# A softmax whose reciprocal sums are multiplied in by the transposing products, and pools that wait by tile

## Chip, cores and metric

The kernel runs on one core of a Trainium2 chip. The metric is the device time of one execution in microseconds (us). The core has five engines that work side by side, each through its own queue in order: TensorE (PE, the matrix products; PEld is its weight load), VectorE (DVE), ScalarE (ACT), GpSimd (POOL) and SyncE (SP, which here issues most transfers). An instruction starts when it is at the head of its queue and the semaphores that it waits for have been raised. Products write to PSUM, eight banks of 128 partitions x 512 fp32 values; DVE and ACT read them from there.

## What is computed

Two small networks over 512 tokens of width 1024, one after the other, in fp32: first a layer of a linear recurrence beside a long convolution, a feed-forward layer, a gated embedding, a windowed attention (16 heads) and again feed-forward and gate; then twice a layer with 8 heads of dilated and 8 of latent attention, followed by a feed-forward layer. The change concerns the softmax of the three attentions:

```python
pr = jax.nn.softmax(s.reshape(B, H, GRID_W, kh * kw), axis=-1)   # windowed
...
p = jnp.exp(s - m)                                               # dilated
l = jnp.sum(p, axis=-1, keepdims=True)
o = jnp.einsum('brhnij,brhnjd->brhnid', p, vw.astype(jnp.float32)) / l
...
p = jax.nn.softmax(s, axis=-1)                                   # latent
return jnp.einsum('bhqk,bkhd->bqhd', p.astype(v.dtype), v)
```

In the kernel the three dilated configurations are one dense attention with a bias that carries the distances, the masks and the weights of the mixture.

## The kernel before

Activations stand transposed, features on partitions and the 512 tokens along a row, as eight tiles `x[k]`. A large product (`gemm`) goes by output tiles of 128 features. For each it loads a weight tile `raw` through SP's queue; ACT rounds it to `wh` (L281), POOL takes the remainder `wl` (L282), and PE adds up three products for each 128 of depth, `wh` by the upper part of x, `wh` by its lower part, `wl` by the upper part (L292 to L294, in fp32r, a form of fp32 that goes over the array once). The result stands in a bank `ps_g`, and an evacuating function on DVE or ACT takes it away.

The stages follow in the order mix, mod, ffn.0, ple.0, na, setup2, ffn.1, ple.1, attn.0, mlp.0, attn.1, mlp.1. `na` is the windowed attention, `attn.0` and `attn.1` the dense layers. Each stage opens a pool of PSUM banks (`banks`, with a number of buffers for each kind: `g` for the large products, `a` for small ones; in attention also `s` scores, `t` transposed tiles, `o` outputs) and a pool in SBUF. A scheduler in the library sets the order on each engine from the order of the code, priorities and its own model of durations; it also makes the semaphores. By default the first tile that lies where an earlier pool lay waits for all of that pool to be released.

One softmax tile has 128 queries on partitions and up to 512 keys along a row. In `head` (dense layers) PE computes the scores into `ps_s`; DVE takes the maximum of each row `mx` (L1684, with the bias, or L1765); `probabilities` follows: DVE negates and scales the maximum (L1416), ACT takes the exponential into `e` and adds up each row into `sm` (L1418), DVE inverts `sm` (L1419), and `e` is multiplied by it, on DVE (L1425) for even tiles and on ACT (L1421) for odd ones. PE then transposes the four 128x128 blocks of `e` with the identity `ident` into `ps_t` (L1583), ACT rounds them to `pth` (L1584), DVE takes the remainder `ptl` (L1585), and PE multiplies with the values into `ps_o`. A dense layer has 16 heads of four such tiles. `na_head` does the same with tiles of 192 or 256 keys and two or three blocks (transposition at L1382), ten blocks a head. Between these PE has fillers: the products that the next heads need, or the output products `out2`. `cast_rows` (L1538) spreads a row of norms over 128 partitions with one product. `rms_of` does the same for the norm of x with a column of reciprocals, the identity as the moving operand (L357).

Of the kernel before, what the change touches and what calls it, by code (L numbers as in the profile page):

```python
# [9 lines left out]
F32 = mybir.dt.float32  # L10
# [7 lines left out]
P = 128  # L18
# [196 lines left out]
class Net:  # L215
    def __init__(self, ctx, tc, ins, at, out):
        self.tc, self.nc, self.ins, self.at, self.out = tc, tc.nc, ins, at, out
        self.bg = []
        pool = lambda name, **k: ctx.enter_context(tc.tile_pool(name=name, bufs=1, **k))
        self.const = pool("const")  # L220
        self.wp = pool("wp")
        self.xp = pool("xp")
        self.dram = pool("dram", space=bass.MemoryType.DRAM)
        nc = self.nc
        self.vecs = self.const.tile([P, ins["vecs"].shape[1]], F32, name="vecs")
        nc.sync.dma_start(self.vecs, ins["vecs"])
        self.ones = self.const.tile([P, P], F32, name="ones")
        nc.vector.memset(self.ones, 1.0)
        self.ident = self.const.tile([P, P], F32, name="ident")
        nc.sync.dma_start(self.ident, ins["ident"])  # L230
        self.weng = nc.gpsimd
        self.nw = 3
        self.ctx = ctx
        self.setup1()

    def make_x(self):
# [19 lines left out]
    @contextmanager  # L256
    def banks(self, **n):

        with self.tc.tile_pool(name="ps", bufs=1, space=PSUM) as self.ps:
            self.nb = n  # L260
            yield

# [113 lines left out]
    def ffn(self, i):  # L376
        nc, tc = self.nc, self.tc
        up, down = self.ins[f"ffn_up{i}"], self.ins[f"ffn_down{i}"]
        NF = DFF // P
        xs = self.scaled_parts(f"ffn_norm{i}")  # L380
        R, _ = self.rms()
        with tc.tile_pool(name=f"ffn{i}", bufs=1) as pool:
            def conv(o, m):
                u = pool.tile([P, S], F32, name="u", bufs=3)
                nc.vector.tensor_mul(u, o, R)
                c = pool.tile([P, S], F32, name="c", bufs=4)
                self.conv3(c, u, f"ffn{i}_c", f"ffn{i}_cb", m)
                return c

            for f0 in range(0, NF, 8):  # L390
                f1 = min(f0 + 8, NF)
                gs, held = [], {}

                def evac(m, o):
                    c = conv(o, m)
                    if m < NF:
                        nc.scalar.activation(c, c, AF.Gelu_apprx_tanh)
                        held[m] = c
                        return
                    gate = held.pop(m - NF)  # L400
                    nc.vector.tensor_mul(c, c, gate)
                    h = pool.tile([P, S], F32R, name="gh", bufs=10)
                    l = pool.tile([P, S], F32R, name="gl", bufs=10)
                    self.split(h, l, c)
                    gs.append((h, l))

                self.gemm(up, [m for f in range(f0, f1) for m in (f, f + NF)], xs, evac, lead=0 if f0 else 4)

                def add(m, o):
                    nc.vector.tensor_add(self.x[m], self.x[m], o)  # L410

                self.gemm(down, range(NKD), gs, add, f0, f1, tick=2)

    def ple(self, i):
        nc, tc = self.nc, self.tc
        with tc.tile_pool(name=f"ple{i}", bufs=1) as pool:
            p = pool.tile([P, 2, S], F32, name="p")
            nc.scalar.dma_start(p, self.ins[f"pT{i}"])
            ph = pool.tile([P, 2, S], F32R, name="ph")
            pl = pool.tile([P, 2, S], F32R, name="pl")  # L420
            self.split(ph, pl, p)
            xs = self.scaled_parts(f"ple_norm{i}")
            R, _ = self.rms()
            prj = {}

            def evac_p(m, o):
                prj[m] = o

            def evac(m, o):
                t = pool.tile([P, S], F32, name="t", bufs=3)  # L430
                nc.vector.tensor_mul(t, o, R)
                nc.scalar.activation(t, t, AF.Sigmoid)
                nc.vector.tensor_mul(t, t, prj.pop(m))
                nc.vector.tensor_add(self.x[m], self.x[m], t)

            psp = [(ph[:, k], pl[:, k]) for k in range(2)]
            for g in (range(2), range(2, 4), range(4, 6), range(6, 8)):
                self.gemm(self.ins[f"ple_proj{i}"], g, psp, evac_p)
                self.gemm(self.ins[f"ple_gate{i}"], g, xs, evac, lead=2)


    def mod(self):
        nc = self.nc
        const = self.ctx.enter_context(self.tc.tile_pool(name="mods", bufs=1))
        act = const.tile([P, NKD], F32, name="c_act")
        nc.scalar.activation(act, self.vecs[:, self.at["c"] : self.at["c"] + NKD], AF.Silu)
        self.mods = [const.tile([P, 6, NKD], F32, name=f"mod{i}") for i in range(2)]
        self.gains = [const.tile([P, 2, NKD], F32, name=f"gain{i}") for i in range(2)]
        self.bgctx = ExitStack()
        self.mpool = self.bgctx.enter_context(self.tc.tile_pool(name="mod", bufs=1))  # L450
        self.bg.append(self.mod_steps(act))
        self.edges()

# [56 lines left out]
    def mlp(self, i):  # L510
        nc, tc = self.nc, self.tc
        xs = self.modulated_parts(i, 1)
        with tc.tile_pool(name=f"mlp{i}", bufs=1) as pool:
            for f0 in range(0, 4 * NKD, NKD):
                gs = []

                def evac(m, o):
                    c = pool.tile([P, S], F32, name="c", bufs=3)
                    nc.scalar.activation(c, o, AF.Relu)  # L519
                    nc.vector.tensor_mul(c, c, c)  # L520
                    h = pool.tile([P, S], F32R, name="gh", bufs=10)
                    l = pool.tile([P, S], F32R, name="gl", bufs=10)
                    self.split(h, l, c)
                    gs.append((h, l))

                self.gemm(self.ins[f"mlp_in{i}"], range(f0, f0 + NKD), xs, evac, lead=0 if f0 else 4)

                def add(m, o):
                    nc.vector.scalar_tensor_tensor(  # L529
                        self.x[m], o, self.mods[i][:, 5, m : m + 1], self.x[m], ALU.mult, ALU.add  # L530
                    )

                self.gemm(self.ins[f"mlp_out{i}"], range(NKD), gs, add, f0, f0 + NKD)


    def mix(self):
# [88 lines left out]
            rw3 = self.rw_out(c, 3, prev, self.pair(3))  # L625
        with self.banks(g=4, a=4):
            self.mix_add(hy, rw3)

    def mix_add(self, hy, rw3):
        nc = self.nc  # L630
# [624 lines left out]
    def na(self):  # L1255
        nc, tc = self.nc, self.tc
        with ExitStack() as ctx:
            pool = ctx.enter_context(tc.tile_pool(name="na", bufs=1))
            raw, rs, sums = {}, {}, {}

            new = lambda: pool.tile([P, S], F32, name="raw", tag="raw", bufs=18)
# [99 lines left out]
    def na_head(self, h, q, k, vh, vl, es, pool):  # L1361
# [7 lines left out]
        for j, (k0, n, o0, b0, kts) in enumerate(self.TQ):  # L1369
# [5 lines left out]
            ev = e[:, k0 - P * kts[0] :][:, :n]  # L1375
            mx = pool.tile([P, 1], F32, name="mx", bufs=8)
            nc.vector.tensor_tensor_reduce(ev, o[:, :n], bias[:, o0 : o0 + n], 1.0, -3e38, ALU.add, ALU.max, mx)
            self.probabilities(ev, ev, mx, 0.125, pool, nc.scalar if j % 2 else nc.vector)
            o = self.psum("t")
            nk = len(kts)  # L1380
            for t in range(nk):
                nc.tensor.transpose(o[:, t * P : (t + 1) * P], e[:, t * P : (t + 1) * P], self.ident)  # L1382
            o = o[:, : nk * P].rearrange("p (t c) -> p t c", c=P)
            b = (0, 1, 4, 7)[j]
            b = slice(b, b + 2 * nk - 1, 2)
# [26 lines left out]
    def probabilities(self, e, s, mx, scale, pool, eng):  # L1412
# [4 lines left out]
        sm = pool.tile([P, 1], F32, name="sm", bufs=8)  # L1417
        nc.scalar.activation(e, s, AF.Exp, scale=scale, bias=nb, accum_out=sm)  # L1418
        nc.vector.reciprocal(sm, sm)  # L1419
        if eng is nc.scalar:  # L1420
            nc.scalar.activation(e, e, AF.Copy, scale=sm)  # L1421
        elif eng is nc.gpsimd:
            eng.tensor_mul(e, e, sm.to_broadcast(list(e.shape)))
        else:
            eng.tensor_scalar(e, e, sm, None, ALU.mult)  # L1425


    def setup1(self):
# [11 lines left out]
    def setup2(self):  # L1440
# [3 lines left out]
        self.sin = c.tile([P, S], F32, name="sin")  # L1444
        self.dbias = self.dram.tile([8, 4, P, S], F32, name="dbias")
        self.bgctx = ExitStack()
        bp = self.bgctx.enter_context(self.tc.tile_pool(name="bias", bufs=1))
        dist = bp.tile([P, 4, S], F32, name="dist")
        ln = bp.tile([P, 896], F32, name="ln")
        nc.scalar.dma_start(ln, self.ins["dil_ln"])  # L1450
# [119 lines left out]
    def head(self, scores, scale, vs, col, pool, put):  # L1570
# [3 lines left out]
        for half in range(2):  # L1574
            pth = pool.tile([P, 2, 4, P], F32R, name="pth", bufs=2)
            ptl = pool.tile([P, 2, 4, P], F32R, name="ptl", bufs=2)
            for jj in range(2):
                s, mx = scores(2 * half + jj)
                e = pool.tile([P, S], F32, name="e", bufs=3)
                self.probabilities(e, s, mx, scale, pool, nc.scalar if jj else nc.vector)  # L1580
                o = self.psum("t")
                for k in range(4):
                    nc.tensor.transpose(o[:, k * P : (k + 1) * P], e[:, k * P : (k + 1) * P], self.ident)  # L1583
                nc.scalar.activation(pth[:, jj], o, AF.Copy)  # L1584
                nc.vector.tensor_sub(ptl[:, jj], o, pth[:, jj].bitcast(F32))  # L1585
            w = slice(half * 256, half * 256 + 256)
# [5 lines left out]
    def attn(self, i):  # L1592
        nc, tc = self.nc, self.tc
        with ExitStack() as ctx:
            pool = ctx.enter_context(tc.tile_pool(name=f"attn{i}", bufs=1))
            raw = {}
            new = lambda: pool.tile([P, S], F32, name="raw", tag="raw", bufs=16)
            pat = {0: 8, 1: 8, 2: 9} | {3 + m: m for m in range(8)}
# [208 lines left out]
```

## Time and profile before

| | us |
|---|---|
| median of three runs | 3389.04 |
| lowest and highest | 3388.92, 3401.41 |
| the profiled execution | 3400.62 |
| its span | 3398.8 |
| PE, DVE, ACT, POOL busy | 3115.1, 1717.6, 1527.6, 1634.7 |

The profile is of one execution. PE's records overlap, since the next product enters the array while the one before drains, so what a product costs in a dense row is the distance from its start to the next start, and a duration is longer than that. PEclk is the granted share of TensorE's full clock.

### The profile page before, as it was taken

Reading aid. Unit: us, or ns where it says so; the run is one execution under the profiler, and the core shown is the slowest. Engines: PE = TensorE matmul, PEld = TensorE weight load, DVE = VectorE, ACT = ScalarE, POOL = GpSimd, SP = SyncE. Lnnn points to the kernel's source line nnn. Section 1 sums busy time; section 2 is a strip of 40 time slices with the busy share of each in tenths; the row PEclk is TensorE's granted clock in tenths of the full one; section 3 lists DMA queues with packets and bytes.
Section 4 is the critical chain, followed back from the end, with each engine's and each line's share of the span. In section 5 each row is a group of like instructions: output and inputs, shape, how many; then the busy total and the mean of one; then the engine's idle time right before and its main releaser. Section 6 shows DMA issues by size and latency. Waiting matters only on the chain. (4 is left out here: it accounts for less than half of the span.)

```text
span 3398.8 us, 45983 instructions
## 1 busy us (share of the span) xinstructions
PE 3115.1 (92%) x16574; PEld 2442.8 (72%) x16574; DVE 1717.6 (51%) x2959; ACT 1527.6 (45%) x2823; POOL 1634.7 (48%) x1354
## 2 busy tenths in 40 slices
PE   6998768878999999998999989998999999989999
PEld 3776556667777777776788866677888766768887
DVE  6465655658786444478453431884222206852222
ACT  5533233334333455565443544875333438763332
POOL 5551311476544554348754545634444436434444
PEclk8998877989999999999999989999999999999999
DMA  4331201376756223234433222412333224213333
GB/s 124 107 91 28 53 21 38 97 262 211 234 180 217 87 89 95 83 88 133 137 99 95 89 84 72 134 34 65 96 95 95 83 79 126 60 40 95 96 96 103
DMA packets 215319, 349.39 MB, mean 103 GB/s; under 512 B 56031, under 2 KB 73119, under 8 KB 215092
## 3 DMA queue, kind: packets, MB, share of 16 engines
q1 hardware_dynamic: 207088, 327.50, 31.6%
q0 software_dynamic: 3680, 11.21, 1.0%
q10 hardware_dynamic: 4324, 7.74, 0.7%
q8 instruction: 131, 2.15, 0.3%
q14 instruction: 96, 0.79, 0.1%
HBM read 310.97 MB, written 25.10 MB: 99 GB/s over the span
## 5 line engine op out<-in xcount | busy, mean ns | idle before, releaser
L282 POOL TENSOR_TENSOR wl<-raw,wh 128x512 fp32r<-128x512 f32 (+2 forms) x874 | 1123.3, 1289 | 1293.8 <-ACT wh L281 1081.3
L281 ACT ACTIVATE wh<-raw 128x512 fp32r<-128x512 f32 (+2 forms) x874 | 522.8, 602 | 1029.1 <-PE ps_g L293 650.4
L292 PE MATMUL ps_g<-x,wh 128*128 128x512 f32 (+1 forms) x2136 | 852.6, 403 | 62.8 <-ACT x L287 18.3
L294 PE MATMUL ps_g<-x,wl 128*128 128x512 f32 (+1 forms) x2136 | 852.3, 402 | 22.4 <-POOL wl L282 21.9
L293 PE MATMUL ps_g<-x,wh 128*128 128x512 f32 (+1 forms) x2136 | 852.8, 399 | 0.0
L292 PEld LDWEIGHTS ps_g<-x,wh 128*128 128x128 f32 (+1 forms) x2136 | 410.3, 193 | 171.0 <-issue 24.2
L294 PEld LDWEIGHTS ps_g<-x,wl 128*128 128x128 f32 (+1 forms) x2136 | 409.4, 192 | 134.3 <-POOL wl L282 34.3
L293 PEld LDWEIGHTS ps_g<-x,wh 128*128 128x128 f32 (+1 forms) x2136 | 410.1, 192 | 102.5 <-issue 15.7
L294 PE MATMUL ps_g<-gh,wl 128*128 128x512 f32 x864 | 341.8, 398 | 4.5 <-POOL wl L282 4.4
L292 PE MATMUL ps_g<-gh,wh 128*128 128x512 f32 x864 | 341.1, 397 | 2.7 <-ACT wh L281 2.1
L293 PE MATMUL ps_g<-gl,wh 128*128 128x512 f32 x864 | 341.6, 396 | 0.7 <-DVE gl L288 0.7
L294 PEld LDWEIGHTS ps_g<-gh,wl 128*128 128x128 f32 x864 | 162.5, 188 | 45.4 <-POOL wl L282 7.7
L292 PEld LDWEIGHTS ps_g<-gh,wh 128*128 128x128 f32 x864 | 162.6, 188 | 42.2 <-ACT wh L281 4.2
L529 DVE SCALAR_TENSOR_TENSOR xr<-ps_g,mod,xr 128x512 f32<-128x512 f32 x64 | 48.1, 751 | 286.3 <-PE ps_g L294 286.3
L293 PEld LDWEIGHTS ps_g<-gl,wh 128*128 128x128 f32 x864 | 162.7, 188 | 39.4 <-DVE gl L288 1.7
L520 DVE TENSOR_TENSOR c<-c 128x512 f32<-128x512 f32 x64 | 88.1, 1376 | 181.6 <-ACT c L519 181.6
L474 DVE SCALAR_TENSOR_TENSOR macc<-wmod,c_act,macc 128x1024 f32<-128x1024 f32 x84 | 135.1, 1608 | 30.3 <-DMA wmod<-in_w_mod 29.7
L287 ACT ACTIVATE gh<-c 128x512 fp32r<-128x512 f32 x108 | 68.2, 631 | 156.6 <-DVE c L520 92.3
L1152 DVE SCALAR_TENSOR_TENSOR c<-u,vecs,c 128x511 f32<-128x511 f32 x88 | 94.5, 1075 | 62.8 <-ACT c L1151 62.7
L288 DVE TENSOR_TENSOR gl<-c,gh 128x512 fp32r<-128x512 f32 x108 | 82.5, 764 | 65.1 <-ACT gh L287 64.9
L345 POOL TENSOR_TENSOR tmp<-tmp 128x512 f32<-128x512 f32 x70 | 96.7, 1382 | 24.6 <-ACT tmp L343 19.8
L292 PE MATMUL ps_o<-pth,vh 128*64 128x256 f32 (+2 forms) x336 | 96.5, 288 | 6.9 <-ACT pth L1584 2.2
(447 smaller groups left out, 5024.9 us busy)
## 6 DMA issues: line engine op xcount, KB each, us to landing
wmod<-in_w_mod SPq DMA_DIRECT2D x96, 512.0 KB
raw<-in_ffn_up SPq DMA_DIRECT2D x176, 256.0 KB
raw<-in_mlp_in SPq DMA_DIRECT2D x128, 256.0 KB
raw<-in_mlp_out SPq DMA_DIRECT2D x128, 256.0 KB
raw<-in_ffn_down SPq DMA_DIRECT2D x80, 256.0 KB
b<-dbias SPq DMA_DIRECT2D x64, 256.0 KB
raw<-in_in_f SPq DMA_DIRECT2D x44, 256.0 KB
raw<-in_ple_gate SPq DMA_DIRECT2D x32, 256.0 KB
```

Source lines behind the costliest of these rows:

```text
L281: nc.scalar.activation(h, raw, AF.Copy)
L282: self.weng.tensor_sub(l, raw, h.bitcast(F32))
L287: nc.scalar.activation(h, src, AF.Copy)
L288: (eng or nc.vector).tensor_sub(l, src, h.bitcast(F32))
L292: nc.tensor.matmul(out, wh, xh, start=first, stop=False)
L293: nc.tensor.matmul(out, wh, xl, start=False, stop=False)
L294: nc.tensor.matmul(out, wl, xh, start=False, stop=last)
L345: nc.gpsimd.tensor_add(sq, sq, acc)
L474: nc.vector.scalar_tensor_tensor(acc, w, act[:, k : k + 1], acc, ALU.mult, ALU.add)
L520: nc.vector.tensor_mul(c, c, c)
L529: nc.vector.scalar_tensor_tensor(self.x[m], o, self.mods[i][:, 5, m : m + 1], self.x[m], ALU.mult, ALU.add)
L1152: nc.vector.scalar_tensor_tensor(c[:, 1:], u[:, : S - 1], self.v(f"{w}w0", m), c[:, 1:], ALU.mult, ALU.add)
```

## The change

`probabilities` no longer multiplies `e`. It makes a 128x128 tile `diag`, the identity with each row multiplied by that row's reciprocal sum, on the engine that multiplied `e` before (DVE for even tiles, ACT for odd ones), in three buffers. The four (or two, three) blocks are no longer transposed: each is the stationary operand of a regular fp32 product with `diag` as the moving one, which gives the transposed block with the factors in it. Beside it, from the end of `mix` on, the PSUM pools and most SBUF pools of the stages are opened with `reuse_waits="tile"`: a new tile waits for the tiles that lay in its own place, not for the whole pool before.

```diff
@@ Net.__init__
+        self.reuse = "pool"
@@ banks
-        with self.tc.tile_pool(name="ps", bufs=1, space=PSUM) as self.ps:
+        with self.tc.tile_pool(name="ps", bufs=1, space=PSUM, reuse_waits=self.reuse) as self.ps:
@@ ffn (the same in ple, mod, mlp, na, setup2 and attn)
-        with tc.tile_pool(name=f"ffn{i}", bufs=1) as pool:
+        with tc.tile_pool(name=f"ffn{i}", reuse_waits="tile", bufs=1) as pool:
@@ mix, at its end
             self.mix_add(hy, rw3)
+        self.reuse = "tile"
@@ na_head (the same in head, with four blocks)
-            self.probabilities(ev, ev, mx, 0.125, pool, nc.scalar if j % 2 else nc.vector)
+            diag = self.probabilities(ev, ev, mx, 0.125, pool, nc.scalar if j % 2 else nc.vector)
             o = self.psum("t")
             nk = len(kts)
             for t in range(nk):
-                nc.tensor.transpose(o[:, t * P : (t + 1) * P], e[:, t * P : (t + 1) * P], self.ident)
+                nc.tensor.matmul(o[:, t * P : (t + 1) * P], e[:, t * P : (t + 1) * P], diag, start=True, stop=True)
@@ probabilities
         nc.vector.reciprocal(sm, sm)
+        diag = pool.tile([P, P], F32, name="diag", bufs=3)
         if eng is nc.scalar:
-            nc.scalar.activation(e, e, AF.Copy, scale=sm)
-        elif eng is nc.gpsimd:
-            eng.tensor_mul(e, e, sm.to_broadcast(list(e.shape)))
+            nc.scalar.activation(diag, self.ident, AF.Copy, scale=sm)
         else:
-            eng.tensor_scalar(e, e, sm, None, ALU.mult)
+            eng.tensor_scalar(diag, self.ident, sm, None, ALU.mult)
+        return diag
```

The lines of the changed kernel stand two or three further down (L292 is L294 there, L1583 is L1586). Up to the first heads of `na` every engine has the order of before, and only waits differ. PE at the start of `ffn.0`, before (the names in brackets are the engines whose semaphores an instruction waits for):

```order
L292 MATMUL ps_g<-x_6342,wh 128x512 [waits DVE_49,Activation_49]
L293 MATMUL ps_g<-x_6342,wh 128x512
L294 MATMUL ps_g<-x_6342,wl 128x512 [waits Pool_49]
L292 MATMUL ps_g<-x_6342,wh 128x512 [waits Activation_49]
L293 MATMUL ps_g<-x_6342,wh 128x512
```

and of the change:

```order
L294 MATMUL ps_g<-x_6342,wh 128x512 [waits DVE_49,Activation_49]
L295 MATMUL ps_g<-x_6342,wh 128x512 [waits DVE_49]
L296 MATMUL ps_g<-x_6342,wl 128x512 [waits Pool_49]
L294 MATMUL ps_g<-x_6342,wh 128x512 [waits Activation_49]
L295 MATMUL ps_g<-x_6342,wh 128x512
```

The first product's wait for DVE was for the last L641 (`x[7]`), the last reader of the old banks; now it is for the L641 of `x[6]`, which read the bank that the new one lies in. The second product now has a wait of its own, for the lower part of the scaled `x[0]`.

PE among the last latent heads of `attn.0`, before (`ps_o` is the product with the values, `x_19510` an input of the output product):

```order
L1583 MATMUL ps_t<-ident,e 128x128 [waits PE_49]
L1583 MATMUL ps_t<-ident,e 128x128 x3
L1583 MATMUL ps_t<-ident,e 128x128 [waits DVE_49,PE_49]
L1583 MATMUL ps_t<-ident,e 128x128 x3
L292 MATMUL ps_s<-hd 128x512 [waits Activation_49]
L293 MATMUL ps_s<-hd 128x512
L294 MATMUL ps_s<-hd 128x512
L292 MATMUL ps_g<-x_19510,wh 128x512 [waits DVE_49]
L293 MATMUL ps_g<-x_19510,wh 128x512
L294 MATMUL ps_g<-x_19510,wl 128x512 [waits Pool_49]
```

and of the change, at the same tiles:

```order
L1586 MATMUL ps_t<-diag,e 128x128 [waits PE_49]
L1586 MATMUL ps_t<-diag,e 128x128 x3
L294 MATMUL ps_s<-hd 128x512 [waits DMAHW0_49,Activation_49]
L295 MATMUL ps_s<-hd 128x512
L296 MATMUL ps_s<-hd 128x512 [waits DMAHW1_49]
L294 MATMUL ps_s<-hd 128x512 [waits Activation_49]
L295 MATMUL ps_s<-hd 128x512
L296 MATMUL ps_s<-hd 128x512
L1586 MATMUL ps_t<-diag,e 128x128 [waits DVE_49,PE_49]
L1586 MATMUL ps_t<-diag,e 128x128 x3
```

The products with `diag` stand where the transpositions stood; two groups of them that followed each other now have score products between them.

PE at the change of banks in `attn.0`, ahead of its first head, before:

```order
L1538 MATMUL ps_a<-rsA,cast 128x512 [waits DVE_49]
L1538 MATMUL ps_g<-rsA,cast 128x512 [waits DVE_49,PE_49]
L1538 MATMUL ps_g<-rsA,cast 128x512
L292 MATMUL ps_g<-x_18219,wh 128x512 [waits DVE_49]
```

and of the change:

```order
L1541 MATMUL ps_a<-rsA,cast 128x512 [waits DVE_49]
L1541 MATMUL ps_g<-rsA,cast 128x512 [waits DVE_49] x2
L294 MATMUL ps_g<-x_18283,wh 128x512 [waits DVE_49,Activation_49]
```

Before, the first broadcast into the new `ps_g` waited for the last split of the values (L288), which freed the last old bank; now each of the two waits for the normalised tile (L1626) whose broadcast lay in its bank.

## Rows read from the trace of the kernel before

**Rows 1.** The page's first part: busy us of each engine, share, instructions.

```profile
PE 3115.1 (92%) x16574; PEld 2442.8 (72%) x16574; DVE 1717.6 (51%) x2959; ACT 1527.6 (45%) x2823; POOL 1634.7 (48%) x1354
```

**Rows 2.** By stretch: us, busy (count) PE, PEld, DVE, ACT, POOL; PEclk, DMA, GB/s.

```profile
1310.00:1520.00 210.00, 197.74 (x1191) 162.03 (x1191) 123.93 (x422) 137.95 (x357) 95.80 (x85) 0.98 0.33 95
...
2125.00:2310.00 185.00, 172.54 (x990) 131.10 (x989) 145.85 (x360) 145.77 (x304) 80.56 (x75) 1.00 0.26 76
...
2828.00:3013.00 185.00, 172.44 (x991) 131.13 (x990) 144.81 (x360) 146.01 (x304) 80.58 (x75) 1.00 0.26 76
```

**Rows 3.** The same view, slices of 10 us in the first dense layer.

```profile
2135.00:2145.00 10.00, 10.00 (x52) 6.84 (x51) 5.73 (x15) 8.30 (x20) 3.42 (x4) 1.00 0.49 134
...
2185.00:2195.00 10.00, 9.59 (x55) 6.65 (x54) 9.97 (x31) 9.21 (x20) 3.58 (x4) 1.00 0.40 118
...
2295.00:2305.00 10.00, 7.01 (x52) 5.74 (x51) 5.04 (x11) 5.29 (x11) 0.00 (x0) 1.00 0.00 0
```

**Rows 4.** Groups by line and shape, PE: count, busy us, mean ns, idle before.

```profile
L1583 PE MATMUL ps_t<-ident,e 128*128 128x128 f32 x512 | 76.1, 274 | 1.5 <-DVE nb L1416 0.9 <-DVE sm L1419 0.4
...
L1382 PE MATMUL ps_t<-ident,e 128*128 128x128 f32 x160 | 27.8, 279 | 2.6 <-DVE ptl L1387 2.0 <-ACT e L1421 0.3 <-DVE sm L1419 0.2
...
L357 PE MATMUL ps_a<-ident,Rc 128*128 128x128 f32 x80 | 15.7, 359 | 5.3 <-DVE Rc L323 5.3
```

**Rows 5.** PE in order of time: start us, us, what, how many in a row.

```profile
1941.48 1.05 PE L357 MATMUL ps_a<-ident,Rc 128*128 128x128 f32 x8
1942.28 0.48 PE L293 MATMUL ps_g<-x,wh 128*128 128x512 f32 x1
...
2127.31 0.60 PE L1583 MATMUL ps_t<-ident,e 128*128 128x128 f32 x4
2127.67 0.49 PE L292 MATMUL ps_g<-x,wh 128*128 128x512 f32 x1
```

**Rows 6.** Busy time by stretch around these two places; PEclk is third from the end.

```profile
1941.00:1943.00 2.00, 2.00 (x14) 1.81 (x13) 0.00 (x0) 0.43 (x1) 0.00 (x0) 1.00 0.42 131
2127.00:2128.00 1.00, 1.00 (x8) 0.82 (x8) 0.97 (x3) 1.00 (x3) 0.92 (x3) 1.00 0.52 174
```

**Rows 7.** Groups by line and shape, DVE and ACT.

```profile
L1425 DVE TENSOR_SCALAR e<-e,sm 128x512 f32<-128x512 f32 x64 | 46.6, 728 | 0.9
...
L1425 DVE TENSOR_SCALAR e<-e,sm 128x192 f32<-128x192 f32 x16 | 6.8, 426 | 0.3
...
L288 DVE TENSOR_TENSOR pt<-ps_g,pt 128x128 fp32r<-128x128 f32 x12 | 3.3, 285 | 0.9 <-ACT pt L287 0.6
...
L681 DVE MEMSET blocks<- 128x128 f32 x1 | 0.2, 165 | 0.1
...
L1421 ACT ACTIVATE e<-e,sm 128x512 f32<-128x512 f32 x64 | 46.1, 720 | 23.7 <-DVE sm L1419 15.3 <-DVE nb L1416 8.2
```

**Rows 8.** Waits of PE from 2125 to 2310: us in total, times, longest.

```profile
PE ps_o L293 <- DVE ptl L1585: 1.9, 5, 0.8
PE ps_s L1681 <- DVE mx L1684: 1.9, 2, 1.3
```

**Rows 9.** In order of time: what ends and begins at four stage starts.

```profile
744.66 3.38 POOL L282 TENSOR_TENSOR wl<-raw,wh 128x512 fp32r<-128x512 f32 x2
...
749.34 0.77 PE L292 MATMUL ps_g<-x,wh 128*128 128x512 f32 x1 [7.91 <-DVE xr L641]
...
1239.14 0.77 PE L292 MATMUL ps_g<-x,wh 128*128 128x512 f32 x1 [7.35 <-DVE t L433]
...
1537.61 0.47 PE L292 MATMUL ps_g<-x,wh 128*128 128x512 f32 x1 [2.73 <-DVE xr L1328]
...
2107.07 0.73 DVE L1626 SCALAR_TENSOR_TENSOR raw<-raw,vecs,ps_a 128x512 f32<-128x512 f32 x1
...
2108.56 1.19 PE L1538 MATMUL ps_g<-rsA,cast 64*128 64x512 f32 x2 [2.60 <-DVE vl L288]
```

**Rows 10.** Waits of PE from 690 us on: the longest in total.

```profile
PE ps_g L294 <- POOL wl L282: 26.2, 30, 7.1
```

More of the change, by code (lines that the diff above doesn't have):

```diff
@@ L415, in ple @@
         nc, tc = self.nc, self.tc
-        with tc.tile_pool(name=f"ple{i}", bufs=1) as pool:
+        with tc.tile_pool(name=f"ple{i}", reuse_waits="tile", bufs=1) as pool:
             p = pool.tile([P, 2, S], F32, name="p")
@@ L449, in mod @@
         self.bgctx = ExitStack()
-        self.mpool = self.bgctx.enter_context(self.tc.tile_pool(name="mod", bufs=1))
+        self.mpool = self.bgctx.enter_context(self.tc.tile_pool(name="mod", reuse_waits="tile", bufs=1))
         self.bg.append(self.mod_steps(act))
@@ L512, in mlp @@
         xs = self.modulated_parts(i, 1)
-        with tc.tile_pool(name=f"mlp{i}", bufs=1) as pool:
+        with tc.tile_pool(name=f"mlp{i}", reuse_waits="tile", bufs=1) as pool:
             for f0 in range(0, 4 * NKD, NKD):
@@ L1257, in na @@
         with ExitStack() as ctx:
-            pool = ctx.enter_context(tc.tile_pool(name="na", bufs=1))
+            pool = ctx.enter_context(tc.tile_pool(name="na", reuse_waits="tile", bufs=1))
             raw, rs, sums = {}, {}, {}
@@ L1446, in setup2 @@
         self.bgctx = ExitStack()
-        bp = self.bgctx.enter_context(self.tc.tile_pool(name="bias", bufs=1))
+        bp = self.bgctx.enter_context(self.tc.tile_pool(name="bias", reuse_waits="tile", bufs=1))
         dist = bp.tile([P, 4, S], F32, name="dist")
@@ L1579, in head @@
                 e = pool.tile([P, S], F32, name="e", bufs=3)
-                self.probabilities(e, s, mx, scale, pool, nc.scalar if jj else nc.vector)
+                diag = self.probabilities(e, s, mx, scale, pool, nc.scalar if jj else nc.vector)
                 o = self.psum("t")
                 for k in range(4):
-                    nc.tensor.transpose(o[:, k * P : (k + 1) * P], e[:, k * P : (k + 1) * P], self.ident)
+                    nc.tensor.matmul(o[:, k * P : (k + 1) * P], e[:, k * P : (k + 1) * P], diag, start=True, stop=True)
                 nc.scalar.activation(pth[:, jj], o, AF.Copy)
@@ L1594, in attn @@
         with ExitStack() as ctx:
-            pool = ctx.enter_context(tc.tile_pool(name=f"attn{i}", bufs=1))
+            pool = ctx.enter_context(tc.tile_pool(name=f"attn{i}", reuse_waits="tile", bufs=1))
             raw = {}
```

## The prediction

> **What bounds the kernel now.** I read the engine shares first: TensorE is busy 3115 of 3399 us, 92%, and no other engine passes 51% [rows 1]. An average says little about three attention stretches, so the next view is the busy time by stretch [rows 2]: the windowed attention (1310 to 1520 us), the heads of the first dense attention layer (2125 to 2310) and of the second (2828 to 3013). In these PE is busy 197.74 of 210, 172.54 of 185 and 172.44 of 185 us. The idle that the profile shows is thus 12.3 + 12.5 + 12.6 = 37.3 us in all, while DVE and ACT each have about 40 us free in a dense layer. Finer slices show that the limit changes within a layer [rows 3]: in 2135:2145 PE is busy all 10 us and DVE only 5.73; in 2185:2195 DVE has 9.97 of 10; in 2295:2305, the last heads, nobody is full and PE has 7.01. So most of the softmax time is PE's, one part is DVE's, and a short end is a chain.
>
> **The products: two records for one.** Today one transposition is one PE record: 512 at L1583 and 160 at L1382 [rows 4], which is what the code issues (2 layers x 16 heads x 4 query tiles x 4; 16 heads x 10). The broadcast at L357 is the nearest thing to the new operation: a regular fp32 product, 128x128 weights, 128 moving columns from `ident`. The code issues 4 for each of 10 norms, 40, and the trace has 80 records [rows 4]. A regular fp32 product therefore runs twice over the array where the transposition runs once. What a group costs is read from the starts, since records overlap: four transpositions start at 2127.31 and the next instruction at 2127.67, 0.36 us; four products start at 1941.48 and the next at 1942.28, 0.80 us [rows 5]. Both stand between fp32r products, and both at the full granted clock, 1.00, which is 2.4 GHz [rows 6]. That is 0.44 us more for each four, and 672 / 4 = 168 fours: **+73.9 us of PE work**, 28.2 in each dense layer (64 fours) and 17.6 in the windowed attention (40). The bounds are 0, if all of it fell into idle, and the full 73.9.
>
> The Trainium skill, "Perfetto Trace Analysis", section "Transposes", says to do a logical transposition as a transpose and not as a standard matmul, because the transpose skips the arithmetic. The two groups above agree with it and give it a size. By that rule alone the change would cost its whole 73.9 us; the sum below also counts what DVE and ACT give back.
>
> **The scalings: what DVE and ACT lose.** Removed are 64 passes of DVE over 128x512 of 728 ns and 64 of ACT of 720 ns in the dense layers, and 32 smaller ones on each in the windowed attention; in their place come as many over 128x128 [rows 7]. The DVE row with 192 columns has 426 ns, an upper bound for 128; the 128x128 memset with 165 ns is a lower one. I take 0.30 us, the size of the 128x128 subtraction (285 ns). For ACT I take the same. Each query tile thus frees about 0.42 us of one of the two engines: 32 x 0.43 = 13.8 us of DVE's 145.85 and 32 x 0.42 = 13.4 of ACT's 145.77 in a layer. The path of one tile does not get shorter: reciprocal to transposed weights loses 0.42 us on DVE or ACT and gains 0.44 on PE. The order of the last heads shows the same places for the products and a different mix of fillers around them; I price that reordering at nothing, since every filler is still PE work that has to be done, and leave it to the range.
>
> So what comes back is only PE's idle. The longest of the waits that make it end with DVE's split of the transposed tile and DVE's maximum [rows 8], that is, with an engine whose queue gets about a tenth lighter while PE's load in a layer rises from 172.5 to 200.7 us. I take three quarters of the 37.3 us as returned, **-28 us**; a quarter stays, because the last heads wait on a chain that keeps its length. The bounds are 0 and -37.3 of what the profile shows as idle.
>
> **The pools that wait by tile.** This is judged by what the first instruction after a change of banks waits for. Four places have a gap there [rows 9]. At 749.34 (start of `ffn.0`) PE sat 7.91 us for DVE's last L641. In the changed order it needs the one before, and its second product waits for DVE's own half of the scaled input. What is late next is POOL's weight remainder, which starts at 744.66 and takes 1.7 us, so the third product could run near 746.4 instead of 750.3: 4 us at most. But the next long stall of this stage, 7.1 us, is for that same POOL row [rows 10], so a part is handed back there. At 1239.14 (start of `na`) the gap is 7.35 us for DVE's L433, and the changed program waits for the same instruction, because the first new bank lies where the last old one did: no gain. At 1537.61 it is 2.73 us; the weights' ACT and POOL halves come next. At 2108.56, and once more in the second layer, it is 2.60 us for the last L288; the two broadcasts there now wait for an L1626 that ends near 2107.8, so under 1 us each. The sum of the four gaps that can shrink, 7.91 + 2.73 + 2 x 2.60 = 15.8 us, is the upper bound and 0 the lower; I take **-5 us**. DVE's and ACT's first writes into the new SBUF pools are released earlier too, but no PE wait of rows 9 ends with them, so they count nothing; if that cover failed, it would show as ACT waits at the stage starts.
>
> **The sum.** 73.9 - 28 - 5 = +41 us. The profiled execution took 3400.6 us (span 3398.8 and 1.8 around it), so it would become 3442. The median of the runs shown is 3389.0, 11.6 lower, and the forecast for a median is **3430 us**.
>
> **The rivals.** (1) *Full price*: PE's waits stay as they are, since they are chains with the same length, and every record is paid: +74, less 5 for the pools, about 3458 us. For it: in the slices with PE at 10 of 10 nothing can be absorbed; against it: 2185:2195, where DVE is the limit. (2) *No change*: beside the idle shown there are stretches in which PE's records overlap loosely and real room is hidden; if these three stretches hold some 55 us of room and the pools give 10, the sum is near +9, some 3398 us. For it: DVE and ACT at 9 to 10 of 10 in a third of each dense layer; against it: PE at 10 of 10 in the rest. (3) *DVE's queue is the limit of the heads*, so its 13.8 us a layer and some 4 in the windowed attention come off the time and PE's 28.2 a layer fit into gaps: 2 x -13.8 - 4 - 5 = -37, near 3352 us. The point from which it decides is idle of at least 28 us a layer; the profile shows 12.5, so this is unlikely. (4) *The pool switch does nothing*, as is already so at 1239.14: +46, within the forecast's own range.
>
> **How the numbers follow.** About 0.5%, 17 us, is what a measurement of this kernel can tell from no change; the borders are 3372 and 3406. The forecast, with (4) inside it, stands for 3408 to 3450 and gets 0.62. Full price, 3450 and above, gets 0.18. No change, 3372 to 3406, gets 0.16, and faster than that 0.04. Slower is thus 0.62 + 0.18 = 0.80, same 0.16, faster 0.04. The range 3397 to 3463 leaves out the faster case, the lower half of the no-change case and the far end of full price, under 2 in 10 together.
>
> **What would show it.** L1583 and L1382 of the changed kernel should have 1024 and 320 records, and a four about 0.80 us to the next start; were it 512 and 0.36, the main term is gone. The diagonals should take 0.2 to 0.4 us. PE's busy time should rise by more than its idle falls in the three stretches, each of the dense layers' heads growing from 185 to about 200 us. The gap at the start of `ffn.0` should shrink by some 4 us, that of `na` stay near 7. The forecast is wrong if the dense layers keep their 185 us with PE over 95% busy (room was hidden), or if they grow by 28 us (nothing came back).

## The result and the profile after

The changed kernel takes 3436.31 us (median of four runs, 3431.03 to 3448.08) where the kernel before, run beside it, has 3392.26 (3388.92 to 3401.41). The ratio of the two is **1.0106, 95% interval 1.0083 to 1.0128**, that is 28 to 43 us more. The medians, of four runs each, stand 44 us apart, just outside of it; the same softmax, run later beside more runs of the kernel before, gave 38 and 39 us (below), so I go by the ratio, 36 us. The forecast was 3430 in a range of 3397 to 3463. The profiled execution has a span of 3435.9 us, 37.1 more than before; the sum had said +41.

The engine shares of the kernel after:

```profile
PE 3175.2 (92%) x17246; PEld 2518.9 (73%) x17246; DVE 1711.0 (50%) x2959; ACT 1512.3 (44%) x2823; POOL 1632.9 (48%) x1354
```

Against [rows 1] PE has 672 records more, one for each product, and is busy 60.1 us longer; DVE and ACT are a little lighter (6.6 and 15.3 us). The groups by line and shape of the kernel after (count, busy us, mean ns, idle before) show the products:

```profile
L1586 PE MATMUL ps_t<-diag,e 128*128 128x128 f32 x1024 | 131.1, 276 | 0.0
...
L1385 PE MATMUL ps_t<-diag,e 128*128 128x128 f32 x320 | 46.9, 282 | 1.1 <-DVE sm L1422 0.6 <-DVE ptl L1390 0.3 <-DVE nb L1419 0.2
```

The view of the tile `diag` in the kernel after gives shortest, middle and longest duration in ns; the last line is DVE's group, with busy us and mean ns:

```profile
L1427 DVE TENSOR_SCALAR diag<-ident,sm x96: 268/288/1324, 1314.4 to 3037.0; 128x128 f32<-128x128 f32 x96
L1425 ACT ACTIVATE diag<-ident,sm x96: 385/400/405, 1315.5 to 3038.6; 128x128 f32<-128x128 f32 x96
...
L1427 DVE TENSOR_SCALAR diag<-ident,sm 128x128 f32<-128x128 f32 x96 | 42.1, 439 | 2.2 <-PE ps_t L1385 0.5
```

And PE in order of time in the first dense layer after (start us, us, what, how many in a row):

```profile
2133.82 1.06 PE L1586 MATMUL ps_t<-diag,e 128*128 128x128 f32 x8
2134.64 0.47 PE L294 MATMUL ps_g<-x,wh 128*128 128x512 f32 x1
...
2137.19 1.05 PE L1586 MATMUL ps_t<-diag,e 128*128 128x128 f32 x8
2138.00 0.48 PE L1684 MATMUL ps_s<-hd 128*128 128x512 f32 x1
```

1024 and 320 records stand where 512 and 160 stood [rows 4], and four products take 0.82 and 0.81 us to the next start, against 0.36 for four transpositions [rows 5]. Each product stands as two records; how often a record goes over the array no run shows, and the price, read from the starts, doesn't need it.

To compare stages, I cut both traces at the same products: the windowed attention and its neighbours (into the start of `ffn.1`), the first dense layer's heads, the second's. Kernel before (us, busy us and count of PE, PEld, DVE, ACT, POOL, then PEclk, DMA share, GB/s):

```profile
1285.60:1550.50 264.90, 247.62 (x1421) 201.13 (x1420) 154.62 (x467) 160.06 (x396) 125.60 (x110) 0.97 0.31 90
2114.20:2322.80 208.60, 196.14 (x1082) 147.92 (x1081) 153.25 (x378) 158.83 (x327) 103.21 (x94) 1.00 0.27 79
2801.00:3050.30 249.30, 225.98 (x1191) 170.71 (x1190) 170.49 (x409) 184.14 (x368) 119.43 (x109) 0.97 0.25 73
```

The same three, kernel after:

```profile
1285.50:1554.10 268.60, 259.55 (x1581) 217.13 (x1580) 148.11 (x460) 157.19 (x389) 124.46 (x108) 0.99 0.31 89
2119.60:2344.50 224.90, 219.12 (x1338) 179.14 (x1337) 149.00 (x378) 151.49 (x327) 101.34 (x94) 1.00 0.26 74
2822.60:3087.50 264.90, 247.43 (x1448) 200.80 (x1447) 167.14 (x409) 176.26 (x368) 117.80 (x109) 0.97 0.24 68
```

They grow by 3.7, 16.3 and 15.6 us, 35.6 of the 37.1. PE's busy time rises by 56.4 us (669.7 to 726.1), its idle falls by 20.8 (53.1 to 32.3). The first figure is too small for the softmax: its stretch ends 16 us into `ffn.1`, where the pools that wait by tile remove a gap and the time is paid back right behind the cut (see "The pools" below). Cut at the last product of `na`, before and after are

```profile
1285.60:1534.48 248.88, 234.33 (x1367) 190.51 (x1365) 141.54 (x441) 152.72 (x383) 116.14 (x103) 0.98 0.31 89
```

```profile
1285.50:1542.17 256.67, 247.62 (x1526) 207.65 (x1525) 139.03 (x441) 153.55 (x383) 116.83 (x103) 0.99 0.30 87
```

which is 7.8 us, and 39.7 for the three; of the idle that fell, 2.7 us are that gap. The place and the size of the loss are thus as forecast. Why it is near 37 and not the 74 of the added work is what the runs below had to tell, and there the prediction's reason was only a small part of it.

### The profile page after: what moved, and what is told of

Read it like the earlier page. It is cut to its first block, busy times and chain, and to the rows that moved or that the text cites. A ratio compares the mean times of both kernels' runs of the same rounds, so it can differ in the third digit from the quotient of the medians.

```text
span 3435.9 us, 47414 instructions
## 1 busy us (share of the span) xinstructions
PE 3175.2 (92%) x17246; PEld 2518.9 (73%) x17246; DVE 1711.0 (50%) x2959; ACT 1512.3 (44%) x2823; POOL 1632.9 (48%) x1354
## 5 line engine op out<-in xcount | busy, mean ns | idle before, releaser
L294 PE MATMUL ps_g<-x,wh 128*128 128x512 f32 (+1 forms) x2136 | 851.7, 403 | 52.9 <-ACT wh L283 18.9
L294 PEld LDWEIGHTS ps_g<-x,wh 128*128 128x128 f32 (+1 forms) x2136 | 410.2, 193 | 158.1 <-ACT wh L283 27.2
L294 PE MATMUL ps_g<-gh,wh 128*128 128x512 f32 x864 | 341.0, 397 | 2.7 <-ACT wh L283 1.5
L294 PEld LDWEIGHTS ps_g<-gh,wh 128*128 128x128 f32 x864 | 162.6, 188 | 41.9 <-ACT wh L283 3.0
L1586 PE MATMUL ps_t<-diag,e 128*128 128x128 f32 x1024 | 131.1, 276 | 0.0
L1586 PEld LDWEIGHTS ps_t<-diag,e 128*128 128x128 f32 x1024 | 123.9, 191 | 6.3 <-PE ps_s L1685 1.7
```

What stands on the lines that cost most here:

```text
L294: nc.tensor.matmul(out, wh, xh, start=first, stop=False)
L1586: nc.tensor.matmul(o[:, k * P : (k + 1) * P], e[:, k * P : (k + 1) * P], diag, start=True, stop=True)
```

## The experiments

All ratios are against the kernel before, run beside each on the same chip (its median there 3401 to 3403 us); us are the ratio less 1, times that.

| run | ratio | 95% interval | us |
|---|---|---|---|
| 1. diagonals and products, pools as before | 1.0114 | 1.0087 to 1.0140 | +39 |
| 2. pools by tile alone | 0.9972 | 0.9956 to 0.9988 | -9.5 |
| 3. products by the identity, e scaled | 1.0125 | 1.0103 to 1.0147 | +43 |
| 4. diagonals made but not used | 1.0002 | 0.9985 to 1.0020 | +1 |
| 5. products by the identity, order held | 1.0143 | 1.0122 to 1.0164 | +49 |
| 6. diagonals made but not used, order held | 0.9974 | 0.9958 to 0.9991 | -9 |
| 7. kernel before in the order for products | 1.0013 | 0.9997 to 1.0028 | +4 |
| 8. half of the products, order held | 1.0066 | 1.0041 to 1.0091 | +22 |
| 9. diagonals and products, order held | 1.0112 | 1.0090 to 1.0134 | +38 |
| 10. pools by tile, another order in `na` | 0.9975 | 0.9959 to 0.9992 | -8.5 |
| 11. PSUM pools by tile | 0.9989 | 0.9971 to 1.0007 | -4 |
| 12. SBUF pools by tile | 0.9997 | 0.9982 to 1.0011 | -1 |

**The change in its parts.** The first run is the change without `reuse_waits="tile"`.

> The change with its pools waiting as before: only the diagonals and the products with them. My theory (the products' price is paid as PE work, a bit over half of it comes back through lighter DVE and ACT queues, and the pools' switch is worth nothing, since what ffn.0 gains at its start it loses at 769.5 us, in a gap of 5.04 us): 35 to 42 us over the kernel before, ratio 1.0105 to 1.0125, the same as the whole change. Rival (the pools' switch gives some 5 us and more, as my sum had it): 42 to 50 us over, ratio 1.0125 to 1.015.

It measured 1.0114, and the whole change 1.0106; the intervals overlap, so beside the products the pools can't be told from nothing. That it lies in my range says nothing for my reason, since the rival of the third run has about the same number.

The second has only the pools:

> The kernel before with only the pools that wait by tile: transpositions and the scaling of e as before. My theory: nothing, within 3 us of the kernel before (ratio 0.999 to 1.001), the gap at the start of ffn.0 smaller by some 5 us and another one later in that stage larger by as much. Rival (the pools are worth what the sum said): 5 us or more faster, ratio 0.9985 or less.

It measured 0.9972: my new theory (nothing) falls, and the sum's -5 us was nearer to it. This kernel is faster than both, and has the same order on every engine as the kernel before.

**Price and relief apart.** In the third run e is scaled as before, and each block is turned by a product with the identity (the line in `head`; `na_head` has the same edit):

```diff
-nc.tensor.transpose(o[:, k * P : (k + 1) * P], e[:, k * P : (k + 1) * P], self.ident)
+nc.tensor.matmul(o[:, k * P : (k + 1) * P], e[:, k * P : (k + 1) * P], self.ident, start=True, stop=True)
```

> The kernel before with each transposition made a regular fp32 product by the identity; e is still multiplied on DVE and ACT, pools as before. So the products' price without any relief. My theory (the relief is what returned half of the price): 55 to 74 us over the kernel before, ratio 1.016 to 1.022. Rival (the relief returned nothing; half of the 74 us fell into room in PE's row that the records of before don't show as idle): about 37 us over, ratio 1.011, as the whole change.

1.0125 is the rival's number, not mine: without any relief of DVE and ACT, 31 of the 74 us were gone already (the interval, 35 to 50 us, leaves out the 55 to 74 that I expected). The fourth has the relief alone:

```diff
-            nc.scalar.activation(e, e, AF.Copy, scale=sm)
+            nc.scalar.activation(diag, self.ident, AF.Copy, scale=sm)
```

(the same on DVE; the blocks are still transposed with `ident`, so the weights are left without their normalisation).

> The kernel before with the scaling of e replaced by the making of the diagonals, and the transpositions kept as they are with the identity, pools as before; the normalisation of the softmax is left out, since nothing reads the diagonals. So the relief of DVE and ACT without the price. My theory: the waits of PE in the heads shrink, 15 to 30 us faster than before, ratio 0.991 to 0.9955. Rival (the relief is worth nothing): within 3 us, ratio 0.999 to 1.001.

1.0002: nothing, and the interval, 5 us faster to 7 slower, leaves out the 15 to 30 that I expected. The theory that the relief paid half of the bill had fallen. But in these runs the scheduler had also laid every queue anew, since it counts with the durations of the edited instructions. So I held the order: the kernel is first traced without the edit, the scheduler's order is read off, and in the edited kernel each instruction is tied behind the one ahead of it in that order, on its own engine, without a semaphore:

```diff
+    for name in order:
+        i = at.get(name)
+        if i is not None:
+            e = str(i.engine)
+            if e in last:
+                tc.add_manual_dep(i, last[e], free, reason="order")
+            last[e] = name
```

No run holds the kernel before to its own order with nothing else changed. What shows that the hold works is that from the first softmax on, every engine of runs 5, 6, 8 and 9 has its records in the order of the kernel before.

**With the order held.** Products by the identity:

> The kernel before with each transposition made a regular fp32 product by the identity, e scaled as before, and every engine's queue held to the order of the kernel before. Without the hold this edit took 44 us more (ratio 1.0125), not the 74 of its work. Theory of the order (the scheduler, which knows the longer products, put the rows into an order that fits them, and that hid the rest): 60 to 74 us over the kernel before, ratio 1.0175 to 1.022. Theory of the room (PE waits in the heads for chains that its own added work doesn't lengthen, and so the work fills those waits in any order): 35 to 48 us, ratio 1.010 to 1.014.

1.0143, 49 us, inside the theory of the room and far from the 74 of the other. Its three stages, cut as above:

```profile
1285.90:1561.00 275.10, 261.34 (x1581) 217.97 (x1580) 154.78 (x466) 162.69 (x395) 124.51 (x110) 0.99 0.30 87
2124.40:2351.60 227.20, 221.47 (x1339) 179.24 (x1338) 154.20 (x379) 160.78 (x327) 102.48 (x94) 1.00 0.26 73
2829.70:3098.10 268.40, 251.50 (x1448) 202.38 (x1447) 172.70 (x409) 185.59 (x368) 118.82 (x109) 0.97 0.24 68
```

They grow by 47.9 us. Idle falls from 53.1 to 36.4, and busy rises by 64.6, less than the 73.9 of the work. The work itself is not smaller: added up over all blocks in the trace, from each record's start to the next start on PE, without the idle, the transpositions of the kernel before have 70.8 us and the products of this run 144.7, which is 73.9 more. So PE's other records got some 9 us cheaper. In the dense layers (5.5 us of it, at the same granted clock) the trace shows one way: the end of a record is modelled, and in front of a wait a record looks longer. In the kernel before a score product in front of a wait counts 0.40 us:

```profile
2206.70 0.40 PE L294 MATMUL ps_s<-hd 96*128 96x512 f32 x1
2207.61 0.63 PE L1583 MATMUL ps_t<-ident,e 128*128 128x128 f32 x4 [0.52 <-DVE nb L1416]
```

and the one in its place in the held run, with no wait behind it, takes 0.22 us to the next start (the turning products stand at L1434 there):

```profile
2225.97 0.39 PE L294 MATMUL ps_s<-hd 96*128 96x512 f32 x1
2226.19 1.05 PE L1434 MATMUL ps_t<-ident,e 128*128 128x128 f32 x8
```

In the windowed attention (3.9 us of it) the granted clock also went from 0.97 to 0.99, which can be the reason as well. PE's waits in the first dense layer of this run (us in total, times, longest):

```profile
PE ps_s L1689 <- DVE mx L1692: 1.1, 2, 0.7
PE ps_o L293 <- DVE ptl L1593: 1.0, 3, 0.4
...
PE ps_s L292 <- ACT e L1418: 0.3, 1, 0.3
```

These are waits of [rows 8] (mx and ptl had 1.9 us each; most lines stand eight further down), and PE's idle in this stretch falls from 12.5 to 5.7 us. In the same order, PE comes later to the instruction that waits, and what it waits for does not come as much later.

Relief alone, order held:

> The kernel before with the diagonals made in place of the scaling of e and nothing reading them (the normalisation is left out), transpositions by the identity, every engine's queue held to the order of before. Without the hold: ratio 1.0002. Theory of the order (the relief is real and the new order ate it): 10 to 30 us faster than before, ratio 0.991 to 0.997. Theory that PE's waits don't hang on the length of these DVE and ACT steps: within 4 us, ratio 0.999 to 1.001.

0.9974, 9 us faster: between the two ranges, nearer to the weak end of what the theory of the order had (0.997), and clear of no change by its interval. Its three stages:

```profile
1290.10:1551.10 261.00, 244.19 (x1421) 198.53 (x1420) 151.26 (x464) 156.22 (x392) 123.49 (x108) 0.99 0.31 92
2114.70:2320.70 206.00, 195.50 (x1083) 147.88 (x1082) 147.41 (x379) 149.80 (x327) 101.91 (x94) 1.00 0.28 80
2798.60:3046.90 248.30, 227.50 (x1191) 173.26 (x1190) 166.46 (x409) 175.29 (x368) 118.17 (x109) 0.95 0.25 73
```

7.5 us shorter in sum. So there is a relief. That the new order ate it in the run without the hold is likely and not shown apart, since the two intervals (0.9985 to 1.0020, 0.9958 to 0.9991) just overlap. Nor are the 9 us those of lighter queues alone: in both of these runs the transposition waits for the exponential only and no longer for the scaling, so each tile's path is shorter too. Both theories hold in part: the room takes a third of the price (25 of 74 us), and the order may take or give some 5 to 10.

The next run asks for the order alone:

> The kernel before in every instruction (transpositions, e scaled), with every engine's queue held to the order that the scheduler gave the kernel with products by the identity. Theory of the order: that order is the better one for PE, 10 to 30 us faster than before, ratio 0.991 to 0.997. Theory of the room: the order is worth nothing or costs a little, within 6 us, ratio 0.998 to 1.002.

1.0013, the interval just reaching no change: with transpositions the order made for products is no better. In its profile the windowed attention has 255.1 us where the kernel before has 264.9, and the two dense stretches have 215.0 and 256.9 for 208.6 and 249.3, so an order can be better in one stage and worse in the others. With products it is worth 1.0143 less 1.0125, some 6 us, which the intervals don't separate.

Half of the products:

> As the first of these, but only the blocks of the even query tiles are turned by products, the odd ones by transpositions as before: half of the added work (64 of 128 fours in the dense layers, 5 of 10 blocks a head in the windowed attention, 36.9 us of PE work). Theory of the room, with room that is used up first: the first half costs less than half of the whole, 6 to 16 us, ratio 1.002 to 1.005. If the room is shared evenly (each added piece loses the same share): 18 to 24 us, ratio 1.0055 to 1.007. Theory of the order: 30 to 37 us, ratio 1.009 to 1.011.

1.0066 is half of 1.0143 within the interval: that fits a share, about a third, that each added piece loses alike. A room that the first pieces use up was to give 1.002 to 1.005, and the interval just reaches that.

Price and relief together, in the order of before:

> The change's softmax (diagonals, products with them) with pools as before and every engine's queue held to the order of the kernel before. If price and relief simply add (1.0143 for the products in this order, 0.9974 for the relief): ratio 1.0105 to 1.0125, some 40 us over. If the added products already fill the waits that the relief would shorten: ratio 1.0135 to 1.015, as for the products alone.

1.0112; 1.0143 and 0.9974 make 1.0117. They add, and the 1.0135 and more of the other theory lies just outside the interval. Here the products wait for their diagonals, so the path of a tile has its length again.

**Something faster, and which pools.** The tenth run takes the kernel before with pools by tile, in an order that the scheduler gave with products in `na` alone:

> A try at something faster than both kernels: transpositions and scaling of e as before, pools that wait by tile (alone: ratio 0.9972), and the queues held to the order that the scheduler gives when the windowed attention's blocks are turned by products; in the profile of the run with that order the windowed attention took 255.1 us where the kernel before took 264.9. If the two gains add: ratio 0.994 to 0.9965. If the order's gain there was the same waits that the pools remove, or chance of one profile: 0.9965 to 0.9985.

0.9975, as the pools alone. In its profile the windowed attention has 250.50 us, where pools alone have 257.80 (the kernel before has 264.90; some 4 us of that difference are the gap in `ffn.1`, paid back behind the cut):

```profile
1289.20:1539.70 250.50, 239.17 (x1420) 195.11 (x1419) 148.10 (x460) 157.42 (x389) 124.88 (x108) 1.00 0.33 96
```

The whole time does not confirm that gain, so pools by tile alone is the kernel to take. Then PSUM and SBUF pools apart:

> The kernel before with only the PSUM pools waiting by tile, the SBUF pools as before; the order on every engine is that of the kernel before, as it is with all pools by tile. My sum counted all of the pools' gain at the changes of banks and nothing for SBUF: then this run has the whole of the 0.9972, ratio 0.9955 to 0.9985. Rival (the SBUF pools, which release transfers and first writes earlier, carry it): ratio 0.999 to 1.001.

> The kernel before with only the SBUF pools waiting by tile, the PSUM pools as before; the order on every engine is that of the kernel before. With all pools by tile the ratio was 0.9972, with the PSUM pools alone 0.9989. If the gains add and SBUF has the rest: ratio 0.997 to 0.9995. If the pools gain only together (the first tile of a stage needs its bank and its SBUF tiles both early): 0.9995 to 1.001.

0.9989 and 0.9997, each within its interval of no change, and 0.9986 together, which the interval of 0.9972 just holds. The first lies in neither of its ranges, the second in that of pools that gain only together; the intervals decide neither. SBUF pools alone give nothing that can be seen. The traces say more of PSUM. At the change of banks inside `na`, at the start of `ple.1` and at the start of each dense layer's heads, PE goes from one product to another in 1.65, 2.46, 4.93 and 4.92 us in the kernel before. With PSUM pools by tile (runs 2, 10 and 11, and the kernel after) it takes 0.74, 1.38, 3.98 and 3.98, within 0.02 us in each, and in none of the others less than 1.65, 2.45, 4.63 and 4.63. Two of the waits that go, in the kernel before:

```profile
1298.77 0.55 PE L1305 MATMUL ps_g<-wh,x 128*128 128x256 f32 x2 [0.84 <-DVE tmp L319]
...
1929.03 0.47 PE L292 MATMUL ps_g<-ph,wh 128*128 128x512 f32 x1 [0.83 <-ACT wh L281]
```

and the first of them still there with SBUF pools alone:

```profile
1304.65 0.55 PE L1306 MATMUL ps_g<-wh,x 128*128 128x256 f32 x2 [0.84 <-DVE tmp L320]
```

That is 3.9 us, all of it PSUM's. Where the rest of the 9.5 (4 to 15 by its interval) comes from, if it is there, stays open.

## Why the prediction was right, and where it was not

**The price of a product** held: two records for one, 0.81 to 0.82 against 0.36 us for four, and 73.9 us over all blocks. The Trainium skill, "Perfetto Trace Analysis", section "Transposes", advises a transpose over a standard matmul; the runs agree in direction, with 1.0125 and 1.0143 for products by the identity.

**The diagonals** were assumed at 0.30 us on both engines. DVE's middle one takes 0.288 us, but some take up to 1.32 and the mean is 0.439, so DVE frees 0.29 us a tile in place of 0.43; ACT's take 0.400, so ACT frees 0.32 in place of 0.42. In the held run with the relief alone DVE and ACT are busy 13.2 and 21.7 us less in the three stages (478.4 to 465.1, 503.0 to 481.3), some 35 us in all. The prediction had 27.2 for each dense layer alone, 54 for both.

**The -28 us for lighter queues** is the step that failed, in its reason. I took it that PE's idle comes back because DVE and ACT get lighter; PE's rising load stands beside it in the same sentence, with no price of its own. The held runs show 49 us for 74 of work without any relief, so 25 come back by the added work falling into waits of PE itself, and only about 9 by relief. Together that is 34 to 36, near the 28 only because two errors offset each other: the relief was put three times too high, and the room left out. That the time came out near the forecast is to that extent luck. The prediction took the idle that the profile shows (37.3 us) for all that could return. The no-change rival had named the other thing, room behind records that overlap loosely, and had only its size wrong: 55 us in the three stretches, where the held run has 25 in all, 17 of it shown as idle and at most 9 behind records that look busy.

**Full price** (rival 1) is refuted by the 49 us of the held products. **DVE as the limit** (rival 3) would have made the relief alone some 30 us faster, and it was 9 (14 at the far end of its interval).

**The pools.** The -5 us lies inside the measured -15 to -4 on the kernel before, but it is not made up as the sum had it. The kernel after, in order of time:

```profile
737.62 0.50 PE L294 MATMUL ps_g<-x,wh 128*128 128x512 f32 x1 [2.47 <-ACT wh L283]
740.46 0.80 PE L295 MATMUL ps_g<-x,wh 128*128 128x512 f32 x1 [2.34 <-DVE x L374]
741.05 0.63 PE L296 MATMUL ps_g<-x,wl 128*128 128x512 f32 x1
...
1238.94 0.79 PE L294 MATMUL ps_g<-x,wh 128*128 128x512 f32 x1 [7.27 <-DVE t L435]
...
1542.17 0.40 PE L296 MATMUL ps_g<-raw,wl 128*128 128x512 f32 x1
1542.41 0.39 PE L294 MATMUL ps_g<-x,wh 128*128 128x512 f32 x1
...
1557.40 0.50 PE L294 MATMUL ps_g<-x,wh 128*128 128x512 f32 x1 [2.50 <-ACT wh L283]
...
1564.20 0.80 PE L294 MATMUL ps_g<-x,wh 128*128 128x512 f32 x1 [5.51 <-ACT wh L283]
...
2113.02 0.50 PE L1541 MATMUL ps_g<-rsA,cast 64*128 64x512 f32 x1 [0.65 <-DVE raw L1629]
2114.28 0.49 PE L1541 MATMUL ps_g<-rsA,cast 64*128 64x512 f32 x1 [0.75 <-DVE raw L1629]
2115.62 0.77 PE L294 MATMUL ps_g<-x,wh 128*128 128x512 f32 x1 [0.85 <-DVE raw L1670]
```

At `ffn.0` 7.91 us became 2.47 and 2.34, the second for DVE's half of the scaled input as said. Counted from the same earlier product (734.4 before, 728.2 after), the third product of the stage comes at 12.9 us in place of 15.9; 4 us was the most that was forecast. At `na` the gap stayed, 7.27 us for 7.35, and for the same DVE step. At the dense layer 2.60 became 0.65 and 0.75 [rows 9], but the next one is 0.85 where it was 0.41, so the heads gain 1 us a layer. At `ffn.1` the gap of 2.73 us at the start is gone: its first product (1542.41) follows the last one of `na` at once. But 56 records on, PE waits for the weights, where it had not waited, 2.50 us, and four products later 5.51 us; at that second place the kernel before has

```profile
1534.48 0.40 PE L294 MATMUL ps_g<-raw,wl 128*128 128x512 f32 x1
...
1556.53 0.80 PE L292 MATMUL ps_g<-x,wh 128*128 128x512 f32 x1 [4.30 <-ACT wh L281]
```

From the last product of `na` to there it is 22.05 us before and 22.03 after: nothing is gained, and both kernels wait there for ACT's rounding of the weights. What `ffn.0` keeps can't be read from one profile. From the same product to the same product, the kernel before and the kernel after:

```profile
734.40:789.50 55.10, 47.19 (x218) 39.04 (x217) 25.98 (x30) 27.20 (x43) 47.08 (x47) 0.94 0.54 184
```

```profile
728.20:791.10 62.90, 53.05 (x219) 43.29 (x218) 33.35 (x33) 28.67 (x45) 48.26 (x48) 0.86 0.49 163
```

That looks like a loss, but the run with pools by tile alone, whose semaphores there are the same, and the one with SBUF pools alone, whose bank waits are those of before, have

```profile
726.70:779.50 52.80, 49.27 (x218) 38.93 (x217) 26.50 (x29) 26.64 (x42) 47.19 (x46) 0.96 0.53 183
```

```profile
734.30:797.10 62.80, 51.93 (x218) 42.81 (x217) 31.94 (x33) 28.60 (x45) 48.26 (x48) 0.86 0.49 162
```

The stage thus comes in a short form (52.8 to 55.5 us in eight of the fourteen profiles, the two kernels' and the twelve runs') and a long one (59.6 to 63.0 in six), with either kind of wait. In the long form PE waits for DVE at the broadcast of the norm, as in the kernel after, and the granted clock of the stretch is 0.86 in the two rows above, where the short form has 0.94 and 0.96:

```profile
774.54 2.08 PE L359 MATMUL ps_a<-ident,Rc 128*128 128x128 f32 x8 [5.04 <-DVE Rc L325]
```

In the kernel before the same broadcast has no wait. All six long profiles have 3.8 to 5.0 us there, three of them among the four with PSUM pools by tile. What decides it was not tried. My reading after the result, that this stage gives back what its start gains, came from one profile, and the measured 0.9972 went against it.

## What to carry to other kernels

A cheap special operation on the engine that bounds the kernel (here a transposition) is not to be traded for a general one that saves time on engines with slack: some 35 us of work taken from DVE and ACT bought about 9, and 74 put on PE cost 49. Added work on a busy engine is not paid in full where its queue has many short waits (here a third was not); look at starts, not at busy time, for the room, and expect a share rather than all or nothing. When stages are compared, cut behind the place where a gained wait could be paid back. Where a scheduler counts durations, hold the order before judging what an edit itself is worth: the run without the hold read the relief as nothing.

## What was not expected

TensorE's granted clock after short idle times went both ways. Busy time by stretch, the kernel before, right after PE had idled 2.73 us at the start of `ffn.1`:

```profile
1537.60:1541.20 3.60, 3.59 (x9) 2.83 (x10) 1.59 (x3) 1.14 (x2) 2.97 (x3) 0.56 0.74 209
```

and the kernel after, further on in the same stage, following 2.50 and then 5.51 us idle:

```profile
1557.40:1558.60 1.20, 1.20 (x4) 0.59 (x4) 1.20 (x2) 1.18 (x2) 1.20 (x2) 0.96 0.08 31
...
1564.20:1567.60 3.40, 3.40 (x8) 2.75 (x9) 3.26 (x5) 3.00 (x4) 3.37 (x3) 0.50 0.29 90
```

After 2.73 and 5.51 us it was near 0.5 (1.2 GHz), after 2.50 us at 0.96 (about 2.4 GHz). PE had been busy ahead of the 2.73 and the 2.50, and had run four products between the 2.50 and the 5.51. The length of the last idle time alone does not tell which level follows: in the run with pools by tile alone, 2.25 us idle, with two products between it and 1.20 us idle, was followed by

```profile
724.85:729.70 4.85, 4.85 (x11) 3.81 (x12) 0.00 (x0) 1.69 (x2) 2.86 (x3) 0.50 0.66 196
```
